# Decayed keys by transposes of scaled keys, the low-rank path's splits moved back, and the inverse's diagonal copies spread out

## The chip, the cores and the metric

The kernel runs on one core of one Trainium2 chip. A core has engines that run side by side, each through its own queue in program order: TensorE (PE in the profile, with its weight loads as PEld), VectorE (DVE), ScalarE (ACT), GpSimd (POOL) and SyncE (SP), which here only issues transfers. TensorE writes into eight banks of accumulators (PSUM), from where VectorE or ScalarE reads the results. The metric is the device time of one execution in microseconds (us), median over runs; lower is better.

## The reference, cut to what matters

The model is a trunk of two layers on 512 positions of 1024 channels: a spatial-gating mixer, a gated feed-forward part with a short convolution, an RWKV-7 mixer, and a second feed-forward part. The change lies in the RWKV-7 mixer:

```python
r = xr @ w_r;  k = xk @ w_k;  v = xv @ w_v
w = -jax.nn.softplus(-(w0 + jnp.tanh(xw @ w1) @ w2)) - 0.5
a = jax.nn.sigmoid(a0 + (xa @ a1) @ a2)
...
decay = jnp.exp(-jnp.exp(heads(w)))
y = wkv7_scan(r_h, decay, k_h, v_h, -kk, kk * a_h)
# step of the scan, per head, state of 64 x 64:
sa = jnp.einsum('bhvk,bhk->bhv', state, a_t)
state = state * w_t[:, :, None, :] + sa[..., None] * b_t[:, :, None, :] + v_t[..., None] * k_t[:, :, None, :]
y_t = jnp.einsum('bhvk,bhk->bhv', state, r_t)
```

There are 16 heads of 64 channels. All is float32 in and out.

## The kernel before, in words

**Arithmetic.** Activations lie with channels on the 128 partitions and the 512 positions along the free axis, so 1024 channels are eight tiles. A large product is split in a high and a low float32r part on each side and done as three matmuls (`mm3`, L311 to L317); `split` (L224 to L239) makes the two parts: ScalarE casts the high one (L234), VectorE subtracts for the low one (L235). Small products are plain float32 matmuls.

**The start of the mixer** is `rwkv_first` (L660 to L723). It computes the low-rank factor of the decay and of `a` for all positions into two accumulators `lw`, then runs four loops `kk` over two input tiles each (L696 to L706), with the receptance weights of the first four output tiles. For each input tile `k` it stores the residual to DRAM (L700), normalizes in place (L701), mixes with the shifted input (`mix`, L647 to L653) and splits the result into `xs[k]`. After the second loop the function `lowrank` (L680 to L691) scales the two accumulators (L683, L684), adds them (L685), takes a tanh of the upper half (L686) and splits both halves into `r.lr` (L690, L691). Then come the other four output tiles in two loops `m` (L711 to L723). `r.lr` is first read in `decay` of the first pair (L853, L855).

**The pairs.** Two heads make one tile of 128 channels, a pair; there are eight (`pairs`, L949 to L974). Time is cut into eight chunks of 64 positions. For each pair `decay` works out the cumulated decay of each chunk (`gt`, its inverse `ei`, and the decay over a whole chunk `gc`), `operands` (L889 to L912) forms `ar`, the decayed queries of both kinds, and `bk`, the two kinds of keys divided by the decay (columns 0 to 63 and 64 to 127 of each chunk; on the lower 64 partitions the first kind is copied behind the second, L912, so that the two heads can have the kinds in opposite order). `products` (L914 to L947) then makes, for two halves of four chunks each, the products of `bk` with `ar` (L928), masks them (L932), copies one quarter into `ti` for the inverse (L933) and stores the rest. At the end it needs the keys times the decay to the chunk's end, with positions and channels exchanged, one per chunk and head. It gets them as a matmul of `bk` with a diagonal matrix `dg` of `gc` (L921, L942), copies them to `bt` (L945) and stores them. Accumulators for `products` come by the names `aux` and `us`, two buffers each, taken in turn; the first of the two heads' results goes to one, the second to the other.

**The inverse.** `invert(g)` (L976 to L1037) inverts, for the four pairs of a half `g`, the unit triangular 64 x 64 matrices of all chunks. It solves the 32 x 32 diagonal blocks on VectorE by 31 steps (L1004, L1005), transposes the blocks (L1010, L1011), copies the inverted diagonal blocks back to `ti` on ScalarE (L1015, four copies), and makes the block off the diagonal by two rounds of 32 x 32 matmuls (L1025 with copies L1035, then L1028 with copies L1037), each in two halves of two portions.

**The scan** (L1160 to L1222) runs over the chunks with `bt`, `ti` and the stored tiles.

**What sets the order.** These parts are Python generators; a `yield` ends a portion. `weave` (L328 to L351) runs the main generator (pairs, later the scan), after each portion as many portions of a side generator (the inverse) and of `fill` as a rate gives. `fill` are the dense projections of keys, values, gates and output, a portion being two input tiles of three matmuls. `issue_after` holds a portion's instructions behind a given instruction on its engine. A scheduler then places the instructions of each engine by order of emission and by its own estimate of when operands and buffers are there, so that an engine's order can differ from the order of the text. On the chip each engine follows that order strictly, and waits where an operand is late.

Of the kernel before, what the change touches and what calls it, by code (L numbers as in the profile page):

```python
# [15 lines left out]
ALU = mybir.AluOpType  # L16
# [4 lines left out]
P = 128  # L21
# [4 lines left out]
C = 64  # L26
NCH = T // C
# [117 lines left out]
class Emit:  # L145
# [514 lines left out]
    def rwkv_first(self, r, ep):  # L660
# [19 lines left out]
        def lowrank():  # L680
            t, u = tmp("lt", 1), tmp("lu", 1, T + 1)
            G.memset(u[:, 0:1], 0.0)
            V.tensor_tensor(t, lw[0], rb, ALU.mult)  # L683
            V.tensor_tensor(u[:, 1:], lw[1], rb, ALU.mult)  # L684
            V.tensor_tensor(t, t, u[:, 0:T], ALU.add)  # L685
            S.activation(t[0:64], t[0:64], AF.Tanh)  # L686

            for j, x in enumerate(r.lr):
                hi, lo = slice(64 * j, 64 * j + 64), slice(64 - 64 * j, 128 - 64 * j)
                S.copy(x[hi], t[hi])  # L690
                V.tensor_tensor(x[lo], t[hi], x[hi].bitcast(F32), ALU.subtract)  # L691


        xs = []
        accs = [self.acc() for _ in range(4)]
        for kk in range(4):  # L696
# [8 lines left out]
            if kk == 1:  # L705
                lowrank()  # L706
        for m in range(4):
# [3 lines left out]
        for m in (0, 2):  # L711
            ws = [self.weights(A["wrb"][m + j]) for j in range(2)]
            if m == 2:
                self.load_l2(0)
            accs = [self.acc() for _ in range(2)]
            for k in range(KT):
                for j in range(2):
                    self.mm3(accs[j], self.wcols(ws[j], k * P, P), xs[k], k == 0, k == KT - 1)
                if m == 2:
                    while len(r.xk) < min(k + 3, KT):  # L720
                        r.xk.append(r.mix(2, len(r.xk)))
            for j in range(2):
                S.copy(r.rt[1][:, m + j, :], accs[j])  # L723

    def rwkv_main(self, r, ctx, gain):
# [3 lines left out]
        H = (h0, h1)  # L729
# [184 lines left out]
        def products(p, u):  # L914


            g, i = divmod(p, 4)
            ar, bk = u.ar, u.bk

            dg = tile_([P, NCH, C], "dg", 1)  # L920
            V.tensor_tensor(dg, self.c("id2", C).unsqueeze(1).to_broadcast([P, NCH, C]), bc(gc[:, p], C), ALU.mult)  # L921
            masks = self.c("masks", P)

            for ch in (slice(0, U), slice(U, NCH)):
# [10 lines left out]
                for hd, o, n, q in ((0, P, P, 0), (0, 2 * P, C, P + C), (1, 0, P + C, C)):  # L935
                    nc.sync.dma_start(std[g][ch, H[hd], i, o:o + n].rearrange("c p t -> p c t"), f[H[hd], :, q:q + n])
                yield
            bt = tile_([P, NCH, 2, C], "bt", BT)
            qs = [self.acc(tag).rearrange("p (c t) -> p c t", t=C) for tag in ("aux", "us")]
            for c in range(NCH):  # L940
                for hd in range(2):
                    nc.tensor.matmul(qs[hd][:, c, :], bk[H[hd], c, C * hd:C * hd + P], dg[H[hd], c, :],  # L942
                                     start=True, stop=True)
            for hd in range(2):
                S.copy(bt[:, :, hd, :], qs[hd])  # L945
            nc.sync.dma_start(btd[:, :, p].rearrange("c p a t -> p c (a t)"), bt.rearrange("p c a t -> p c (a t)"))
# [29 lines left out]
        def invert(g):  # L976
# [35 lines left out]
            yield  # L1012
            off = blocks("tt")
            for rows, cols in Q:
                S.copy(tg[rows, :, cols], y[rows])  # L1015
            for i in range(2):
                for hf in range(2):
                    ps = self.acc("aux").rearrange("p (u t) -> p u t", t=32)
                    us = slice(16 * hf, 16 * hf + 16)
                    for u in range(16):  # L1020
                        for hd in range(2):
# [5 lines left out]
                            else:  # L1027
                                nc.tensor.matmul(ps[b0, u, :], off[b1, n, :], y[b1, n, :], start=True, stop=True,  # L1028
                                                 tile_position=(b1.start, b0.start))
                        if u % 8 == 7:  # L1030
                            yield
                    for hd in range(2):
# [353 lines left out]
```

## Time and profile before

| | |
|---|---|
| median of three runs | 1292.31 us (1291.89 to 1294.6) |
| profiled execution, its own time | 1294.26 us |
| its span, first to last instruction | 1292.4 us |
| mean granted TensorE clock | 0.988 |
| TensorE busy | 98% |
| VectorE busy | 66% |
| ScalarE busy | 49% |

A row of a view by line has the line of the kernel, engine, operation, the tile written, an arrow, the tiles read, how many, then the shortest, median and longest duration in ns, the first and last start in us, and shapes. TensorE rows show weights rows*columns and then the streamed operand. A row of the timeline begins with start and duration in us; in square brackets at its end stands how long the engine had been idle before it, and which instruction ended that. Durations of matmuls contain their latency, so that the time that one costs is read from the distance between two starts. Lines are those of the kernel before.

### The profile page before, as it was taken

What the parts mean: (1) busy time and instruction counts of PE and PEld (TensorE: products, weight loads), DVE (VectorE), ACT (ScalarE), POOL (GpSimd) and SP (SyncE); (2) the same over time, 40 slices, a digit from 0 to 9 for tenths busy, and PEclk for the clock granted to TensorE, in tenths of its full rate; (3) what the DMA queues carried; (4) which work ended last, traced back from release to release, by engine and by line L of the source; (5) the groups of instructions that cost most, each with busy time, mean ns of one, the idle gap of its engine ahead of it and who ended that gap; (6) DMA issues with size and microseconds to landing.
All of it is one profiled execution on the core that took longest, in us unless ns stands there. A gap on an engine that the chain in (4) does not pass through costs nothing.

```text
span 1292.4 us, 19533 instructions
## 1 busy us (share of the span) xinstructions
PE 1269.4 (98%) x7591; PEld 1018.9 (79%) x7591; DVE 852.8 (66%) x1401; ACT 631.3 (49%) x1084; POOL 97.7 (8%) x119
## 2 busy tenths in 40 slices
PE   9999999999999999999999998999999999999997
PEld 6878888888888888787777776677888888888886
DVE  6465468888886444765889587765677777763233
ACT  5534456555554333565785645532544444442222
POOL 4100100000000000000000022231100000000001
PEclk9999999999999999999999998999999999999998
DMA  7332457777557764236878699764233333333332
GB/s 252 102 98 83 129 172 256 245 245 242 175 171 220 217 206 151 90 106 185 224 199 239 171 215 227 193 168 144 78 104 98 98 97 96 93 93 98 90 90 78
DMA packets 115452, 201.65 MB, mean 156 GB/s; under 512 B 21600, under 2 KB 53600, under 8 KB 115360
## 3 DMA queue, kind: packets, MB, share of 16 engines
q10 hardware_dynamic: 39104, 112.87, 29.0%
q1 hardware_dynamic: 76256, 87.54, 23.4%
q8 instruction: 59, 0.97, 0.3%
q14 instruction: 33, 0.27, 0.1%
HBM read 152.93 MB, written 47.45 MB: 155 GB/s over the span
## 4 chain that ended last, share of the span: by engine, by line
PE 88%; DVE 5%; ACT 1%; POOL 0%; issue 0%; DMA 0%; DVEq 0%; ACTq 0%; POOLq 0%
PE mm L315 10%; PE mm L316 9%; PE mm L317 9%; PE aux L315 6%; PE aux L317 6%; PE aux L316 6%; PE e L316 6%; PE e L315 6%; PE e L317 5%; PE us L317 5%; PE us L315 5%; PE us L316 5%; PE aux L928 1%; PE aux L942 1%; PE us L1186 1%; PE us L1199 1%
## 5 line engine op out<-in xcount | busy, mean ns | idle before, releaser
L234 ACT CAST w<-w 128x512 fp32r<-128x512 f32 x340 | 206.3, 610 | 374.3 <-PE aux L317 94.8
L235 DVE TENSOR_TENSOR w<-w,w 128x512 fp32r<-128x512 f32 x340 | 233.3, 688 | 196.7 <-ACT w L234 196.2
L315 PE MATMUL mm<-mxh,w 128*128 128x512 f32 (+1 forms) x416 | 171.7, 414 | 1.6 <-ACT mxh L234 1.6
L316 PE MATMUL mm<-mxl,w 128*128 128x512 f32 (+1 forms) x416 | 166.7, 401 | 0.2 <-DVE mxl L235 0.2
L317 PE MATMUL mm<-mxh,w 128*128 128x512 f32 (+1 forms) x416 | 166.3, 400 | 0.0
L342 POOL TENSOR_TENSOR ss<-ss,sq 128x512 f32<-128x512 f32 x30 | 41.0, 1368 | 777.6 <-issue 595.1
L315 PEld LDWEIGHTS mm<-mxh,w 128*128 128x128 f32 (+1 forms) x416 | 78.2, 189 | 22.0 <-issue 3.3
L317 PEld LDWEIGHTS mm<-mxh,w 128*128 128x128 f32 (+1 forms) x416 | 78.7, 189 | 18.1 <-issue 1.2
L316 PEld LDWEIGHTS mm<-mxl,w 128*128 128x128 f32 (+1 forms) x416 | 78.9, 190 | 16.3 <-issue 1.1
L539 ACT ACTIVATE cv<-z,par 128x512 f32<-128x512 f32 x88 | 71.7, 817 | 28.8 <-DVE z L537 23.8
L315 PE MATMUL us<-mxh,w 128*128 128x512 f32 x216 | 84.6, 392 | 0.0
L315 PE MATMUL aux<-mxh,w 128*128 128x512 f32 x216 | 84.5, 391 | 0.0
L317 PE MATMUL aux<-mxh,w 128*128 128x512 f32 x216 | 84.2, 390 | 0.3 <-DVE w L235 0.3
L316 PE MATMUL aux<-mxl,w 128*128 128x512 f32 x216 | 84.1, 389 | 0.0
L316 PE MATMUL us<-mxl,w 128*128 128x512 f32 x216 | 84.1, 389 | 0.0
L317 PE MATMUL us<-mxh,w 128*128 128x512 f32 x216 | 84.1, 389 | 0.0
L315 PE MATMUL e<-mxh,w 128*128 128x512 f32 x208 | 81.5, 392 | 2.5 <-ACT mxh L234 2.4
L316 PE MATMUL e<-mxl,w 128*128 128x512 f32 x208 | 81.2, 390 | 0.1
L317 PE MATMUL e<-mxh,w 128*128 128x512 f32 x208 | 81.0, 389 | 0.0
L540 DVE SCALAR_TENSOR_TENSOR cv<-z,par,cv 128x512 f32<-128x512 f32 x88 | 66.1, 752 | 19.9 <-ACT cv L539 19.9
L541 DVE SCALAR_TENSOR_TENSOR cv<-z,par,cv 128x512 f32<-128x512 f32 x88 | 66.0, 752 | 2.9
L315 PEld LDWEIGHTS e<-mxh,w 128*128 128x128 f32 x208 | 39.1, 188 | 11.3 <-ACT mxh L234 3.3
(1088 smaller groups left out, 2605.1 us busy)
## 6 DMA issues: line engine op xcount, KB each, us to landing
w<-in_wup ACTq DMA_DIRECT2D x88, 512.0 KB, 3.7
w<-in_wdn ACTq DMA_DIRECT2D x32, 512.0 KB, 3.6
st<-std SPq DMA_DIRECT2D x30, 320.0 KB, 6.9
w<-wkd ACTq DMA_DIRECT2D x16, 512.0 KB, 5.0
w<-wvd ACTq DMA_DIRECT2D x16, 512.0 KB, 5.7
w<-wod ACTq DMA_DIRECT2D x16, 512.0 KB, 4.3
w<-in_wdn ACTq DMA_DIRECT2D x16, 384.0 KB, 3.4
w<-in_wsu ACTq DMA_DIRECT2D x8, 512.0 KB, 3.7
```

The source lines that it names most:

```text
L234: nc.scalar.copy(hi[r, :n], src)
L235: (lo_eng or nc.vector).tensor_tensor(lo[r, :n], src, hi[r, :n].bitcast(F32), ALU.subtract)
L315: mm(acc, wh, xh, start=first, stop=False)
L316: mm(acc, wh, xl, start=False, stop=False)
L317: mm(acc, wl, xh, start=False, stop=last)
L342: nc.gpsimd.tensor_tensor(self.ss, self.ss, self.sq, ALU.add)
L539: nc.scalar.activation(c, z[:, 2:], AF.Identity, scale=cw(2, i), bias=self.p("conv_b", l * 44 + i))
L540: nc.vector.scalar_tensor_tensor(c, z[:, 1:T + 1], cw(1, i), c, ALU.mult, ALU.add)
L541: nc.vector.scalar_tensor_tensor(c, z[:, 0:T], cw(0, i), c, ALU.mult, ALU.add)
L928: nc.tensor.matmul(qs[hd][:, c - ch.start, :], bk[H[hd], c, C * hd:C * hd + P], ar[H[hd], c, :], start=True, stop=True)
L942: nc.tensor.matmul(qs[hd][:, c, :], bk[H[hd], c, C * hd:C * hd + P], dg[H[hd], c, :], start=True, stop=True)
L1186: nc.tensor.matmul(us[H[hd], 0, i, :], ar(i, hd, 0), vu[:, hd, i, :], start=True, stop=True)
```

## The change

There are three edits.

1. `lowrank` becomes a generator. Its first portion (L682 to L684) stays after the second loop `kk`. The sum, tanh and the first split follow after input tile 2 of the next stage's first loop (`m == 0`), the second split after tile 4.
2. In `products` the diagonal `dg` and its 16 matmuls go. Instead VectorE scales `bk` by `gc` into a tile `be`, for four chunks at a time, ScalarE copies one kind of key behind the other on the lower partitions, as for `bk`, and TensorE transposes `be`, chunk by chunk and head by head, against the identity. The scaling of the first half stands at the start of `products`; its transposes and the scaling of the second half stand at the end of the first half; the transposes of the second half stand after the loop. The accumulators of the transposes are taken after the first half.
3. In `invert` the four copies L1015 no longer stand together ahead of the matmuls; one follows each of the four portions of the first round.

```diff
+            yield
             V.tensor_tensor(t, t, u[:, 0:T], ALU.add)
             S.activation(t[0:64], t[0:64], AF.Tanh)
...
                 S.copy(x[hi], t[hi])
                 V.tensor_tensor(x[lo], t[hi], x[hi].bitcast(F32), ALU.subtract)
+                yield
...
-        xs = []
+        xs, low = [], lowrank()
...
             if kk == 1:
-                lowrank()
+                next(low)
...
+                if m == 0 and k in (2, 4):
+                    next(low)
...
-            dg = tile_([P, NCH, C], "dg", 1)
-            V.tensor_tensor(dg, self.c("id2", C).unsqueeze(1).to_broadcast([P, NCH, C]), bc(gc[:, p], C), ALU.mult)
+            id2, qb = self.c("id2", C), []
+
+            def decayed(ch):
+
+                be = tile_([P, U, 3 * C], "be", 1)
+                V.tensor_tensor(be[:, :, 0:P], bk[:, ch, 0:P], bc(gc[:, p, ch], P), ALU.mult)
+                S.copy(be[h1, :, P:], be[h1, :, 0:C])
+                return be
+
+            def turned(ch, be):
+                for c in range(U):
+                    for hd in range(2):
+                        nc.tensor.transpose(qb[hd][:, ch.start + c, :], be[H[hd], c, C * hd:C * hd + P], id2[H[hd]])
+
+            be = decayed(slice(0, U))
...
-                yield
+                if not qb:
+                    qb[:] = [self.acc(tag).rearrange("p (c t) -> p c t", t=C) for tag in ("aux", "us")]
+                    turned(ch, be)
+                    be = decayed(slice(U, NCH))
+                yield
+            turned(slice(U, NCH), be)
             bt = tile_([P, NCH, 2, C], "bt", BT)
-            qs = [self.acc(tag).rearrange("p (c t) -> p c t", t=C) for tag in ("aux", "us")]
-            for c in range(NCH):
-                for hd in range(2):
-                    nc.tensor.matmul(qs[hd][:, c, :], bk[H[hd], c, C * hd:C * hd + P], dg[H[hd], c, :],
-                                     start=True, stop=True)
             for hd in range(2):
-                S.copy(bt[:, :, hd, :], qs[hd])
+                S.copy(bt[:, :, hd, :], qb[hd])
...
-            off = blocks("tt")
-            for rows, cols in Q:
-                S.copy(tg[rows, :, cols], y[rows])
+            off, own = blocks("tt"), iter(Q)
...
                         if u % 8 == 7:
+                            if i == 0:
+                                rows, cols = next(own)
+                                S.copy(tg[rows, :, cols], y[rows])
                             yield
```

## The prediction

> **What bounds the kernel now.** First the page: its header, the busy times and the chain of waits.
>
> ```profile
> span 1292.4 us, 19533 instructions
> PE 1269.4 (98%) x7591; PEld 1018.9 (79%) x7591; DVE 852.8 (66%) x1401; ACT 631.3 (49%) x1084; POOL 97.7 (8%) x119
> PE 88%; DVE 5%; ACT 1%; POOL 0%; issue 0%; DMA 0%; DVEq 0%; ACTq 0%; POOLq 0%
> ```
>
> TensorE is occupied for 98% of the span and carries 88% of the chain, so what is taken off TensorE comes off the end, unless another engine is late at that place. The whole-span shares hide that, so the second view is the table of stretches (duration, then PE, PEld, DVE, ACT, POOL busy with instruction counts, the granted TensorE clock, DMA share, GB/s).
>
> ```profile
> 600.00:680.00 80.00, 80.00 (x636) 61.82 (x635) 65.94 (x115) 58.64 (x110) 0.56 (x5) 1.00 0.78 216
> 680.00:700.00 20.00, 19.86 (x152) 15.49 (x151) 18.16 (x46) 12.10 (x27) 0.11 (x1) 0.91 0.76 216
> 700.00:723.00 23.00, 22.54 (x150) 16.99 (x146) 21.77 (x51) 10.77 (x24) 0.61 (x2) 1.00 0.97 272
> 600.00:723.00 123.00, 122.39 (x933) 94.30 (x931) 105.86 (x211) 81.51 (x159) 1.28 (x8) 0.99 0.81 227
> 723.00:740.00 17.00, 16.94 (x303) 14.30 (x303) 6.44 (x9) 11.51 (x18) 0.00 (x0) 0.94 0.47 122
> ```
>
> The eight pairs run from 600 to 740. TensorE is full throughout, but VectorE is at 65.94 of 80 up to 680 (14.1 us free), 18.16 of 20 after it, and 21.77 of 23 in 700 to 723 (1.2 us free), where it also runs the first inverse's substitution. There VectorE sets the pace as much as TensorE.
>
> **The decayed keys: TensorE's part.** The change removes 16 products of keys with a diagonal per pair (L942) and adds 16 transposes. By line, all over the span, with the nearest transposes the kernel has (L1239: 32 of them, so one record each, where the 128 products of L942 make 256 records, two each):
>
> ```profile
> L942 PE MATMUL aux<-dg,bk x128: 218/272/320, 615.9 to 736.6; 64*128 64x64 f32 x128
> L942 PE MATMUL us<-dg,bk x128: 218/272/320, 615.9 to 736.4; 64*128 64x64 f32 x128
> L1239 PE MATMUL aux<-cst,y x32: 271/273/328, 773.4 to 887.2; 128*128 128x128 f32 x32
> 615.88 0.32 PE L942 MATMUL aux<-dg,bk 64*128 64x64 f32 x1
> 617.81 0.51 PE L315 MATMUL mm<-mxh,w 128*128 128x512 f32 x1
> 773.43 0.60 PE L1239 MATMUL aux<-cst,y 128*128 128x128 f32 x4
> ```
>
> One pair's 32 records hold TensorE from 615.88 to 617.81: 1.93 us, 0.060 a record, since the two heads' records run side by side; eight pairs make 15.4. The new 128 transposes have the same weights' shape (64 rows, 128 columns) and the same two heads. At one record each and the same 0.060 they take 7.7, so 7.7 is saved. The trace shows no transpose on half the rows: if two heads' transposes do not run side by side, each costs what an L1239 one does, (0.60 - 0.27)/3 = 0.11 us, 128 of them 14.1, and only 1.3 is saved. The value 0.060 is taken, because the shape is that of L942 and only the identity differs.
>
> A group of 64-row instructions also pays at its edges:
>
> ```profile
> 621.44 0.39 PE L316 MATMUL mm<-mxl,w 128*128 128x512 f32 x1
> 621.67 0.39 PE L317 MATMUL mm<-mxh,w 128*128 128x512 f32 x1
> 621.99 0.37 PE L928 MATMUL aux<-ar,bk 64*128 64x128 f32 x1
> 622.20 0.27 PE L928 MATMUL aux<-ar,bk 64*128 64x128 f32 x1
> 622.31 0.27 PE L928 MATMUL aux<-ar,bk 64*128 64x128 f32 x1
> ```
>
> The last dense product before it takes 0.32 to the next start and not 0.23, the first pair of records 0.21 and not 0.11; with as much at the end (I assume symmetry) it is some 0.38 a group. The single group becomes two half groups, each following a group of L928 in program order. Both standing alone cost 8 x 0.38 = 3.0 more, both joined to L928 give 3.0 back; I take nothing. TensorE saves 7.7, bounds 1.3 - 3.0 = -1.7 (a loss) and 10.7.
>
> The trace agrees on the records with the Trainium skill, "TensorE: Matmul & The Clock Gate", section Terms: it gives the chip's transpose mode as four times faster for FP32. By that 15.4 would fall to an estimated 3.9 and 11.6 be saved; the spacing of 0.11 at L1239 does not show so much, so I stay with the half.
>
> **Its cost on VectorE and ScalarE.**
>
> ```profile
> L921 DVE TENSOR_TENSOR dg<-cst,gc x8: 684/685/693, 601.3 to 716.1; 128x512 f32<-128x512 f32 x8
> L933 ACT COPY ti<-lq x32: 392/404/408, 607.5 to 734.1; 64x256 f32<-64x256 f32 x32
> L932 DVE TENSOR_TENSOR lq<-us,cst x16: 646/681/692, 607.4 to 729.9; 128x512 f32<-128x512 f32 x16
> L945 ACT COPY bt<-aux x8: 562/586/587, 617.9 to 736.9; 128x512 f32<-128x512 f32 x8
> ```
>
> The diagonal (0.685) goes; two scalings of 4 chunks x 128 columns, again 128x512, come: 8 x 0.685 = 5.5 us more on VectorE. Two copies of 64x256 a pair come on ScalarE: 16 x 0.404 = 6.5. ScalarE has 41 us free in 600 to 723 and hides them. VectorE has 123 - 105.9 = 17.1 free, 14.1 of it before 680; five pairs' 3.4 us are hidden there by TensorE's dense products. After 680 they are not: of the two pairs around 690 to 716 TensorE's saving (2 x 0.96 = 1.9) is lost, because VectorE has next to nothing free there, and 2 x 0.685 = 1.4 is added. The DMA share of 0.97 there speaks the same way: the weights could hardly come sooner. Net of the transposes: 7.7 - 1.9 - 1.4 = 4.4 us gained; if the cover also fails before 680, 3.4 less and the rest of the saving with it.
>
> The accumulators are held longer: the transposes' two stay from the first half of a pair to its end, so the second half's products wait for the masks on the first half (L932, two of 0.68), and the next pair's first products for the copies out (L945, two of 0.59). With one buffer for the scaled keys, VectorE's second scaling waits for the first transposes, and the next operand work queues behind it. Dense products between these places cover them, as the second pair shows, whose second half starts after the masks on the first have ended:
>
> ```profile
> 623.38 0.68 DVE L932 TENSOR_TENSOR lq<-aux,cst 128x512 f32<-128x512 f32 x1
> 623.98 0.68 DVE L932 TENSOR_TENSOR lq<-us,cst 128x512 f32<-128x512 f32 x1
> 625.75 0.37 PE L928 MATMUL aux<-ar,bk 64*128 64x128 f32 x1
> ```
>
> So they are costed at nothing; uncovered they are 1.4 + 1.2 = 2.6 us a pair.
>
> **The low-rank path.** TensorE's one long wait before the pairs, with VectorE's row of work in front of it:
>
> ```profile
> 545.02 0.39 PE L317 MATMUL aux<-mxh,w 128*128 128x512 f32 x1
> 547.81 0.50 PE L315 MATMUL e<-mxh,w 128*128 128x512 f32 x1 [2.40 <-ACT mxh L234]
> 540.02 0.68 DVE L685 TENSOR_TENSOR lt<-lt,lu 128x512 f32<-128x512 f32 x1
> 541.83 0.68 DVE L235 TENSOR_TENSOR w<-w,w 128x512 fp32r<-128x512 f32 x1
> 543.00 1.39 DVE L691 TENSOR_TENSOR lr<-lt,lr 64x512 fp32r<-64x512 f32 x2 [0.50 <-ACT lr L690]
> 544.42 1.42 DVE L701 SCALAR_TENSOR_TENSOR h<-h,par,rb 128x512 f32<-128x512 f32 x2
> 541.71 1.26 ACT L690 CAST lr<-lt 64x512 fp32r<-64x512 f32 x2
> ```
>
> From 545.02 to 547.81 is 2.79 us where 0.23 is normal: 2.56 lost. TensorE waits for xs[4], whose first step is L701 at 544.42, queued behind L691, which waited for ScalarE's L690. The change takes L685, the tanh and L690/L691 away from there. VectorE's last work then ends at 541.83 + 0.68 = 542.51 and L701 starts 1.9 us earlier, 2.56 if the split moves up by L685's 0.68 as well. I take 2.2. The two pieces (L685, then L691 in two parts: 2.07 us of VectorE, and tanh and L690, 1.9 of ScalarE) go between dense products of the next loop, which cover them; their reader is the first pair's decay, after two loops of dense products. Bounds: 0, if they stall the next splits as they stall these, and 2.56. No DMA is among them.
>
> **The inverse's copies.** In the second inverse ScalarE has L1015 in front of the operand that TensorE waits for:
>
> ```profile
> 796.73 0.69 DVE L1047 SCALAR_TENSOR_TENSOR sq<-h,omu,sq 128x512 f32<-128x512 f32 x1
> 796.87 1.04 ACT L1015 COPY ti<-li 32x1024 f32<-32x1024 f32 x1 [1.51 <-DVE li L1011]
> 797.82 0.61 ACT L234 CAST mxh<-sq 128x512 fp32r<-128x512 f32 x1
> 798.48 0.72 PE L315 MATMUL mm<-mxh,w 128*128 128x512 f32 x2 [1.56 <-ACT mxh L234]
> ```
>
> Its input is ready at 797.42, the cast starts at 797.82. Later copies free 0.4; one copy's 1.04 either way bounds it, as a copy may now stand in front of another reader.
>
> **The sum.** 2.2 + 4.4 + 0.4 = 7.0 us. The profiled execution took 1294.26 us (1.9 around its span of 1292.4), which gives 1287.3. It was 1.95 slower than the median of the runs, 1292.31, which the new median will be compared with: 1285.3, forecast 1285.5.
>
> **The rivals.**
>
> *VectorE is the bound in all pairs.* For: 14.1 us free before 680 are spread over waits that TensorE's order makes. Against: 3.4 needed. Then transposes bring nothing and 2.6 remains: 1289.7, up to 1291 with the 1.4.
>
> *The transposes are not cheaper* (no side by side, edges paid): -1.7 and -1.4, against 2.6: 1292.8.
>
> *A slow spell of the clock goes.* With small instructions packed, the clock was halved for what followed:
>
> ```profile
> 734.57:737.99 3.42, 3.42 (x76) 3.18 (x68) 0.66 (x1) 1.08 (x3) 0.00 (x0) 1.00 0.37 90
> 737.99:748.23 10.24, 10.24 (x86) 8.08 (x86) 2.14 (x1) 6.13 (x11) 2.36 (x4) 0.50 0.65 156
> ```
>
> In 737.99 to 748.23 it is 0.50, which costs 5.1 us. Before it lie small products, the last pair's L942 among them; with half as many records dense work moves in. Then 1280.2. Against: the inverse's 32-row products stay.
>
> *Slower by the accumulators:* the waits of 2.6 us a pair stand on TensorE because its order puts the second half right behind the first. It decides from 0.9 us a pair on, which eats the 7.0; in full 8 x 2.6 = 20.8 - 7.0: slower by 13.8, at half by 3.4, 1296. Against: in the second pair 1.09 us lie between the masks' end at 624.66 and the second half.
>
> *Slower by the clock:* transposes count little as work, and a spell of 3.41 us at 0.50 follows in each pair, 1.7 us: from four pairs on nothing is gained; eight make 13.6 - 7.0 = 6.6, 1299. The rows above bear it out as far as full occupation (3.42 of 3.42) did not keep the clock. The Trainium skill, "TensorE: Matmul & The Clock Gate", Part 4, says just this of transposes: they do not count as busy as other products do. Against: in a pair dense products surround them, and L942's group left the clock at 1.00 up to 680.
>
> **How the numbers follow.** Forecast 0.52 (1282 to 1289.5), spell gone 0.17, VectorE 0.10, transposes dear 0.05 with 0.05 for mixtures that end near 1291, accumulators 0.06, clock 0.05. The runs tell no change from one of 0.2%, 2.6 us: faster is below 1289.7, slower above 1294.9. Faster: 0.52 + 0.17 + half of VectorE's = 0.74; same 0.15; slower 0.11. The range 1278.5 to 1292 leaves out the last two, part of the dear transposes and little below.
>
> **What would show it.** One record per transpose, and pairs of them 0.11 to 0.12 apart; the wait at 547.81 gone or under 0.7; the first pairs closer together by some 0.7 us each, the last two not; no wait of TensorE's products for L932 or L945 over 0.5. Two records per transpose, or the clock at 0.50 inside the pairs, would make the prediction wrong.

## The result

The changed kernel takes 1299.68 us (median of 11 runs, 1296.19 to 1306.66). The kernel before, run beside it, takes 1292.31 us (median of 11, 1291.23 to 1296.61). The ratio is 1.0052, with a 95% interval of 1.004 to 1.0064: the change made the kernel slower by half a per cent, where 1285.5 us and faster had been forecast, and 1299.68 lies above the range's end of 1292.

The profiled execution after took 1300.81 us, 6.55 more than the one before (1294.26). Of the changed kernel's page, the header, the busy times and the chain by engine:

```profile
span 1299.0 us, 19310 instructions
PE 1273.2 (98%) x7463; PEld 1017.7 (78%) x7463; DVE 857.4 (66%) x1409; ACT 638.2 (49%) x1100; POOL 98.7 (8%) x119
PE 86%; DVE 5%; ACT 2%; DMA 1%; issue 1%; POOL 0%; DVEq 0%; ACTq 0%; POOLq 0%
```

TensorE has 128 records fewer (7463 for 7591), as 256 became 128, yet it is occupied for 3.8 us longer, and its share of the chain fell from 88% to 86%. So TensorE's work did not shrink, and some waits are new. Where they are, the table of stretches of the changed kernel says (duration; PE, PEld, DVE, ACT, POOL busy with counts; granted clock; DMA share; GB/s):

```profile
540.00:548.00 8.00, 7.98 (x35) 6.07 (x34) 8.00 (x14) 5.14 (x10) 0.00 (x0) 1.00 0.28 74
600.00:680.00 80.00, 78.88 (x525) 57.60 (x523) 63.16 (x110) 57.82 (x110) 0.56 (x5) 0.96 0.73 199
680.00:700.00 20.00, 18.06 (x128) 13.17 (x127) 16.46 (x38) 12.99 (x27) 0.11 (x1) 0.98 0.65 181
700.00:723.00 23.00, 23.00 (x124) 17.55 (x124) 18.65 (x42) 12.98 (x30) 0.61 (x2) 0.87 0.77 217
600.00:723.00 123.00, 119.94 (x774) 88.33 (x772) 98.27 (x189) 83.79 (x165) 1.29 (x8) 0.94 0.73 200
```

In the low-rank path's stretch, 540 to 548, TensorE is now full: the stall there is gone. In the pairs it is the other way. In the same 123 us TensorE gets through 774 records instead of 933, 159 fewer where the change itself takes at most 128 away, and VectorE has become *less* busy, 98.3 instead of 105.9: by its share it is not the bound. TensorE is at 18.06 of 20 in 680 to 700, and the weights' transfers fell back with it (200 GB/s instead of 227).

The landmarks place the loss. The first copy of the receptance's first loop, right behind the low-rank path, starts at 554.4 and not 557.4; here are these rows by line, first of the kernel before, then of the changed one (shortest, median, longest in ns, then first and last start):

```profile
L708 ACT COPY rt<-e x1: 587/587/587, 557.4 to 557.4; 128x512 f32<-128x512 f32 x1
```

```profile
L710 ACT COPY rt<-e x1: 589/589/589, 554.4 to 554.4; 128x512 f32<-128x512 f32 x1
L902 DVE TENSOR_TENSOR ar<-kn,gt x8: 651/685/693, 590.7 to 702.4; 128x512 f32<-128x512 f32 x8
L961 ACT COPY bt<-aux x8: 562/576/593, 615.6 to 744.1; 128x512 f32<-128x512 f32 x8
```

L902 opens the operands of each pair, L961 closes the pairs. Before, the first pair's operands began at 593.8, the last one's at 696.7, and the last `bt` copy started at 736.9. So the change was 3.0 us ahead at the first pair, 5.7 us behind at the last one, and 7.2 behind at the end of the pairs.

To see what that time consists of, I kept a ledger for the stretch from the first pair's operands to the scan's first copy of V. From the time that passes, three things are taken: the loss by halved clock (half the length of each spell at a granted clock of 0.50), the time that TensorE idled, and 0.2275 us for each of the 290 dense products in it, which is the distance between the starts of two dense products in a row. The rest is what the *small* products cost TensorE: their own time, the edges of their groups, and the gaps that the profile doesn't count as idle.

| us | passes | halved clock | TensorE idle | 290 dense products | small products |
|---|---|---|---|---|---|
| before | 156.56 | 6.83 | 0.67 | 65.98 | 83.1 |
| after | 162.81 | 6.83 | 5.02 | 65.98 | 85.0 |

The loss in this stretch, 6.25 us, is 4.35 of new idle time and 1.9 of small products, which were to become 7.7 cheaper. Halved clock takes the same 6.83 us in both. The largest waits in the 5.02 us of idle time are 1.7 for a scaling (L928) and 1.6 for a copy on ScalarE that belongs to another part of the mixer (L839). The sum over the whole span closes: -3.04 up to the first pair, +6.25 here, +3.38 in the scan, where 6.8 us more at half the clock (13.65 against 6.83) cost 3.4, and -0.04 behind it make 6.55.

### Why the transposes are not cheap

By line, the changed kernel's transposes (two rows, one for each head's accumulator), the scaling that feeds them and its copy:

```profile
L935 PE MATMUL aux<-cst,be x64: 216/223/273, 604.6 to 739.3; 64*128 64x64 f32 x64
L935 PE MATMUL us<-cst,be x64: 215/223/273, 609.4 to 740.3; 64*128 64x64 f32 x64
L928 DVE TENSOR_TENSOR be<-bk,gc x16: 662/690/694, 598.3 to 738.1; 128x512 f32<-128x512 f32 x16
```

One record per transpose and 0.69 us for a scaling are as forecast. But the first head's transposes begin at 604.6 and the second head's at 609.4. TensorE's timeline of the changed kernel, at one pair's half and around the place of its longest wait:

```profile
612.61 0.39 PE L317 MATMUL mm<-mxh,w 128*128 128x512 f32 x1
612.92 0.46 PE L935 MATMUL aux<-cst,be 64*128 64x64 f32 x4
613.32 0.50 PE L315 MATMUL mm<-mxh,w 128*128 128x512 f32 x1
613.65 0.40 PE L316 MATMUL mm<-mxl,w 128*128 128x512 f32 x1
...
614.22 0.46 PE L935 MATMUL us<-cst,be 64*128 64x64 f32 x4
...
691.37 1.16 PE L944 MATMUL aux<-ar,bk 64*128 64x128 f32 x8
692.46 1.13 PE L841 MATMUL mm<-rt,wb 128*128 128x512 f32 x2
693.52 0.46 PE L935 MATMUL us<-cst,be 64*128 64x64 f32 x4
693.82 1.11 PE L944 MATMUL us<-ar,bk 64*128 64x128 f32 x8
696.63 0.46 PE L935 MATMUL aux<-cst,be 64*128 64x64 f32 x4 [1.71 <-DVE be L928]
```

A row with x4 is four records in a row with nothing of the other head between them. The two heads no longer stand side by side: the first head's four transposes at 612.92 are followed by dense work, the second head's four come at 614.22. Such a group of four costs TensorE 0.58 us over the dense products around it (612.61 to 613.65 is 1.04 for two dense products' 0.46). A pair has four such groups, 2.3 us, where the old single group of 32 records had 1.93, or 2.1 when its edges are counted in the same way (in the pair at 659.18, 2.59 with two dense products). So nothing is saved. The products of keys and queries came apart in the same way: eight records of one head at 691.37 take 1.09 us to the next start, as long as sixteen with the heads side by side (610.26 to 611.36 in the same trace).

I counted in the traces, as lone, each record beside which none of the other head starts within 25 ns. Before, 40 of 256 product records and 34 of 256 records of L942 were lone; after, 128 of 256 and 112 of the 128 transposes (14 of the 16 half groups; in the other two the heads do stand side by side).

### The profile page after: what moved, and what is told of

Its sections match the earlier page's. It is cut to its first block, busy times and chain, and to the rows that moved or that the text cites. A ratio compares the mean times of both kernels' runs of the same rounds, so it can differ in the third digit from the quotient of the medians.

```text
span 1299.0 us, 19310 instructions
## 1 busy us (share of the span) xinstructions
PE 1273.2 (98%) x7463; PEld 1017.7 (78%) x7463; DVE 857.4 (66%) x1409; ACT 638.2 (49%) x1100; POOL 98.7 (8%) x119
## 4 chain that ended last, share of the span: by engine, by line
PE 86%; DVE 5%; ACT 2%; DMA 1%; issue 1%; POOL 0%; DVEq 0%; ACTq 0%; POOLq 0%
PE mm L315 9%; PE mm L316 9%; PE mm L317 9%; PE aux L315 6%; PE aux L317 6%; PE aux L316 6%; PE e L316 6%; PE e L315 6%; PE e L317 6%; PE us L316 5%; PE us L315 5%; PE us L317 5%; PE aux L944 1%; PE e L889 1%; PE us L1216 1%; PE us L1203 1%
## 5 line engine op out<-in xcount | busy, mean ns | idle before, releaser
L317 PEld LDWEIGHTS aux<-mxh,w 128*128 128x128 f32 x216 | 40.6, 188 | 9.3 <-DVE w L235 0.8
```

The lines of the kernel that those rows point to most:

```text
L317: mm(acc, wl, xh, start=False, stop=last)
```

## The experiments

Each run's time was also freed of the clock: less (1 - mean granted clock) times its span, the median of this over the runs. It supposes that the span follows the clock, and with a clock given to 0.001 one run is good to about 0.65 us. What the clock costs is, below, the median less this figure. "Before" was run beside each set and came to 1292.31, 1293.83 (beside e1, e2, e4 and e5), 1293.18 (e3, e6, e7) and 1292.77 us (e8, e9, e10). Without the clock's loss the last three are 1278.0, 1278.7 and 1278.55, so that the clock costs the kernel before 14.2 to 15.8 us.

| kernel | median us | ratio to before (95%) | without clock loss | lone products, of 256 | lone transposes, of 128 (diagonal products, of 256) |
|---|---|---|---|---|---|
| before | 1292.31 | 1 | 1278.0 to 1278.7 | 40 | (34) |
| after | 1299.68 | 1.0052 (1.004 to 1.0064) | 1282.3 | 128 | 112 |
| e1_lowrank | 1290.55 | 0.9979 (0.9967 to 0.9991) | 1275.7 | 40 | (34) |
| e2_turn | 1305.64 | 1.0101 (1.0087 to 1.0116) | 1284.5 | 128 | 112 |
| e3_inverse | 1291.07 | 0.9984 (0.9974 to 0.9994) | 1279.0 | 36 | (34) |
| e4_heads | 1298.78 | 1.0047 (1.0035 to 1.0059) | 1277.6 | 78 | 8 |
| e5_end | 1290.41 | 0.9988 (0.9968 to 1.0007) | 1274.8 | 36 | 16 |
| e6_placed | 1294.74 | 1.0016 (0.9994 to 1.0038) | 1279.2 | 46 | (54) |
| e7_pool | 1302.93 | 1.0066 (1.0048 to 1.0085) | 1278.3 | 38 | 20 |
| e8_unscaled | 1290.11 | 0.9975 (0.9966 to 0.9984) | 1272.8 | 78 | 16 |
| e9_aside | 1298.23 | 1.0039 (1.0026 to 1.0052) | 1277.0 | 72 | 22 |
| e10_both | 1287.27 | 0.9952 (0.9939 to 0.9965) | 1275.7 | 36 | (34) |

The ledger of the pairs, as above, of the profiled executions that are spoken of below (290 dense products, 65.98 us, in each but e6 and e9, which have 291 and 294):

| us | passes | halved clock | TensorE idle | small products |
|---|---|---|---|---|
| before | 156.56 | 6.83 | 0.67 | 83.1 |
| after | 162.81 | 6.83 | 5.02 | 85.0 |
| e4_heads | 159.15 | 8.53 | 7.01 | 77.6 |
| e5_end | 151.38 | 3.41 | 10.40 | 71.6 |
| e6_placed | 152.85 | 0 | 2.38 | 84.3 |
| e7_pool | 159.64 | 10.24 | 11.34 | 72.1 |
| e8_unscaled | 154.27 | 8.53 | 4.72 | 75.0 |
| e9_aside | 158.75 | 10.24 | 7.76 | 73.9 |
| e10_both | 151.06 | 0 | 1.30 | 83.8 |

### One edit at a time: e1_lowrank, e2_turn, e3_inverse

Each is the kernel before with one of the three edits, exactly as the change has it.

```diff
# e1_lowrank: the three hunks of lowrank and rwkv_first alone
+            yield
             V.tensor_tensor(t, t, u[:, 0:T], ALU.add)
...
+                if m == 0 and k in (2, 4):
+                    next(low)
# e2_turn: the hunks of products alone
-            dg = tile_([P, NCH, C], "dg", 1)
...
+            be = decayed(slice(0, U))
...
+            turned(slice(U, NCH), be)
# e3_inverse: the hunks of invert alone
+                            if i == 0:
+                                rows, cols = next(own)
+                                S.copy(tg[rows, :, cols], y[rows])
```

> The kernel before with the first edit alone (low-rank path in three portions). Both theories: the wait of 2.4 us at the start of the mixer goes, as it does in the trace after; 1289.3 against 1292.3 before. If what the later stages lose comes from the shift in time of everything behind (other phase of the clock's halving) and not from the transposes, this kernel loses it too and stands at 1295 or more.

> The kernel before with the second edit alone (transposes of scaled keys). If the transposes carry the whole loss, 1299.7 + 3.0 = 1302 to 1303, and about 112 of 128 transpose records and about 128 of 256 product records run without the other head's record beside them, as in the trace after (before: 34 and 40 of 256). If the loss came with the other two edits: 1292 or less.

> The kernel before with the third edit alone (the inverse's diagonal copies between the portions). All theories: within 0.2% of before, 1291 to 1296; the first edit gave 0.21% and the second cost 1.01%, the change as a whole cost 0.52%, so if the edits simply add, this one would have to give 0.28%, 1290.

Each is taken against the kernel before beside it. The low-rank edit brings 0.2% (2.3 us without the clock's loss), the inverse's copies 0.2% in the runs, but nothing once the clock is taken out (+0.3). The transposes cost 1.0%, 12 us, 6.5 of it at full clock. The three differences at full clock add up to +4.5 (-2.3 + 6.5 + 0.3), and the changed kernel's own is +3.6 to +4.3 (1282.3 against 1278.0 to 1278.7). So, as far as the rounding tells, the edits don't hinder each other, and the whole loss comes with the transposes.

### The two heads held together: e4_heads

The changed kernel, with the transposes of a half held behind the first one of the second head (its operand comes last), so that the heads alternate. No other line changes.

```diff
             def turned(ch, be):
+                with ExitStack() as behind:
                 for c in range(U):
-                    for hd in range(2):
+                    for hd in (1, 0):
                         nc.tensor.transpose(qb[hd][:, ch.start + c, :], be[H[hd], c, C * hd:C * hd + P], id2[H[hd]])
+                        if c == 0 and hd == 1:
+                            behind.enter_context(tc.issue_after(self.last(mybir.EngineType.PE)))
```

> The changed kernel, with each half's eight transposes held behind the first one of the second head, so that the two heads' transposes go side by side. Theory 'heads apart': some 112 lone records at 0.10 become pairs, and 36 groups become about 16 at 0.38 a group: 5 us or more back, 1294 to 1295. Theory 'accumulators held': the products of keys and queries stay as split as they are (128 lone records), 1298 to 1300. Theory 'VectorE': no change, 1299.7.

TensorE's timeline of this kernel, where a half's transposes begin:

```profile
609.06 0.39 PE L317 MATMUL mm<-mxh,w 128*128 128x512 f32 x1
609.38 0.27 PE L936 MATMUL us<-cst,be 64*128 64x64 f32 x1
609.38 0.27 PE L936 MATMUL aux<-cst,be 64*128 64x64 f32 x1
609.49 0.22 PE L936 MATMUL us<-cst,be 64*128 64x64 f32 x1
609.49 0.22 PE L936 MATMUL aux<-cst,be 64*128 64x64 f32 x1
...
609.68 0.33 PE L947 MATMUL us<-ar,bk 64*128 64x128 f32 x1
609.68 0.33 PE L947 MATMUL aux<-ar,bk 64*128 64x128 f32 x1
```

Now eight transposes take 609.38 to 609.68, 0.30 us, and the products right behind them run in pairs too. With dense products on both sides eight take 0.40 us (613.48 to 613.88), the same as four of one head alone took. Lone transposes fell from 112 to 8, lone products from 128 to 78. Without the clock's loss the kernel is 4.6 us faster than the changed one, and in the ledger the small products went from 85.0 to 77.6. So it is shown that the heads' coming apart costs about this much. The measured median is another matter: 1298.78 is only 0.9 below the changed kernel, with overlapping intervals and short of the 1294 to 1295 expected, since this version loses 21 us to the clock where the changed one loses 17.4. In the profiled executions, of the 7.4 us gained on small products 2.0 go to more idle time of TensorE (7.0 us in the stretch), 1.7 to more halved clock in the stretch and 3.4 to more halved clock in the scan.

### All transposes at the end, accumulators taken only there: e5_end

The keys are scaled in place behind each half's products, and all 16 transposes of a pair stand in one group behind both halves, as the old products with the diagonal did; the accumulators are taken there. As in e4 the group is held behind the second head's first transpose, and here the chunks are taken from the last to the first. So this run changes the place, the tile and the order together.

```diff
-                be = tile_([P, U, 3 * C], "be", 1)
-                V.tensor_tensor(be[:, :, 0:P], bk[:, ch, 0:P], bc(gc[:, p, ch], P), ALU.mult)
-                S.copy(be[h1, :, P:], be[h1, :, 0:C])
+                V.tensor_tensor(bk[:, ch, 0:P], bk[:, ch, 0:P], bc(gc[:, p, ch], P), ALU.mult)
+                S.copy(bk[h1, ch, P:], bk[h1, ch, 0:C])
...
-            def turned(ch, be):
...
+            def turned():
+                with ExitStack() as behind:
+                    for c in reversed(range(NCH)):
+                        for hd in (1, 0):
+                            nc.tensor.transpose(qb[hd][:, c, :], bk[H[hd], c, C * hd:C * hd + P], id2[H[hd]])
+                            if c == NCH - 1 and hd == 1:
+                                behind.enter_context(tc.issue_after(self.last(mybir.EngineType.PE)))
...
-            be = decayed(slice(0, U))
...
-                if not qb:
-                    qb[:] = [self.acc(tag).rearrange("p (c t) -> p c t", t=C) for tag in ("aux", "us")]
-                    turned(ch, be)
-                    be = decayed(slice(U, NCH))
+                decayed(ch)
                 yield
-            turned(slice(U, NCH), be)
+            qb[:] = [self.acc(tag).rearrange("p (c t) -> p c t", t=C) for tag in ("aux", "us")]
+            turned()
```

> The changed kernel, with the keys scaled in place after their half's products, and all 16 transposes of a pair in one group at the end, where alone their accumulators are taken. VectorE and ScalarE do the same work as in the changed kernel. Theories 'heads apart' and 'accumulators held': both the lone transposes and the lone products go back to the number before (34 to 40), and the saving shows: one group of 8 pairs of records, 0.9 + 0.38 against 2.2 us a pair, 7 us, with the 3.0 of the low-rank path: 1283 to 1287. Theory 'VectorE' (5.5 us more work where it is the bound): 1297 to 1300. Theory 'clock' (transposes do not count as work): the clock is halved inside the pairs still.

TensorE's timeline of this kernel, from a group's first to its last records and the product behind it:

```profile
613.92 0.27 PE L934 MATMUL us<-cst,bk 64*128 64x64 f32 x1
613.93 0.27 PE L934 MATMUL aux<-cst,bk 64*128 64x64 f32 x1
614.03 0.22 PE L934 MATMUL us<-cst,bk 64*128 64x64 f32 x1
...
614.42 0.22 PE L934 MATMUL us<-cst,bk 64*128 64x64 f32 x1
614.57 0.88 PE L889 MATMUL e<-cst,n 128*64 128x128 f32 x12
```

Sixteen transposes take 0.65 us, pairs of them 0.063 apart: where the heads do stand side by side, a transpose costs 0.03 to 0.04, where the prediction took 0.060, and a pair's 16 a third of the 1.93 us before. In the ledger the small products fall by 11.5 us (83.1 to 71.6), more than the 7.7 forecast: the transposes are cheaper than priced, and the products of keys and queries have kept their partners (36 lone). But the stretch passes only 5.2 us sooner, and 3.4 of that is the clock's: TensorE idles 10.4 us instead of 0.67. Its stretches show where:

```profile
600.00:723.00 123.00, 112.60 (x869) 85.24 (x869) 110.14 (x215) 85.90 (x170) 1.29 (x8) 0.97 0.78 220
640.00:665.00 25.00, 19.98 (x147) 15.38 (x145) 22.01 (x37) 20.03 (x38) 0.11 (x1) 0.86 0.55 142
```

TensorE is busy 19.98 of 25 us in 640 to 665, with VectorE at 22.01. The longest single wait there, in the waits of TensorE from 580 to 750 (what waited, for what, total us, times, longest), is for a step of `decay`, which prepares a later pair:

```profile
PE e L881 <- ACT sq L871: 5.3, 2, 5.0
```

So with the transposes cheap, TensorE runs ahead and meets the other engines' pace; over all, e5 ties with the kernel before (0.9988, interval 0.9968 to 1.0007) although it has the low-rank gain in it, and misses the 1283 to 1287 expected.

### The accumulators alone: e6_placed

The kernel before, with its old products with the diagonal, but in two halves at the change's places, and so with the accumulators held from the first half on. No edit of the other two.

```diff
+            def turned(ch):
+                for c in range(ch.start, ch.stop):
+                    for hd in range(2):
+                        nc.tensor.matmul(qb[hd][:, c, :], bk[H[hd], c, C * hd:C * hd + P], dg[H[hd], c, :],
+                                         start=True, stop=True)
...
+                if not qb:
+                    qb[:] = [self.acc(tag).rearrange("p (c t) -> p c t", t=C) for tag in ("aux", "us")]
+                    turned(ch)
                 yield
+            turned(slice(U, NCH))
```

> The kernel before, its products with the diagonal kept, but taken in two halves at the places where the changed kernel has its transposes, into accumulators held from the end of the first half. No scaled keys, no more VectorE or ScalarE work. Theory 'accumulators held': half of the records lose their partner here too (100 or more lone product records of 256, before 40) and the time is 1298 to 1303. Theory 'heads apart through the copy of one head's keys': both heads' operands are ready together, so pairs stay pairs and only the one more group a pair is paid, 3 us: 1295 to 1297. Theory 'VectorE': as before, 1292 to 1294.

The runs are 0.16% slower, an interval that holds 1, and 0.5 to 1.2 us slower at full clock, which the clock's rounding can make. Lone records hardly rise (46 and 54). So neither the halves nor the held accumulators part the heads. What remains is readiness: the operands of the two heads come ready one after the other, since ScalarE's copy (L929) stands before the second head's, and the diagonal products needed only `bk` and `dg`, which are ready long before. That last step is argued, and the changed kernel's trace bears it out only in part. Of its 14 half groups that came apart, five have the first head's transposes start before the copy for the second head had ended. In the other nine the copy too had ended before either head's transposes began, as for the group at 612.92, whose copy ended at 611.14:

```profile
610.74 0.40 ACT L929 COPY be<-be 64x256 f32<-64x256 f32 x1 [0.93 <-DVE be L928]
```

There nothing forced the heads apart at run time on this account: the order of the instructions was already so. Why the scheduler placed them so, by its own estimate of when operands are there or for another reason, no run shows. Shown are that holding for the later head joins the heads, and that accumulators don't part them.

### What TensorE meets once the transposes are cheap: e7_pool, e8_unscaled, e9_aside

All three are e5_end with one thing changed: the scaling given to GpSimd; the scaling and its copy left out, so that undecayed keys are transposed; the scaling and copy done, but into a tile that nobody reads, the undecayed keys being transposed.

```diff
# e7_pool
-                V.tensor_tensor(bk[:, ch, 0:P], bk[:, ch, 0:P], bc(gc[:, p, ch], P), ALU.mult)
+                G.tensor_tensor(bk[:, ch, 0:P], bk[:, ch, 0:P], bc(gc[:, p, ch], P), ALU.mult)
# e8_unscaled
-                decayed(ch)
# e9_aside
-                V.tensor_tensor(bk[:, ch, 0:P], bk[:, ch, 0:P], bc(gc[:, p, ch], P), ALU.mult)
-                S.copy(bk[h1, ch, P:], bk[h1, ch, 0:C])
+                be = tile_([P, U, P], "be", 1)
+                V.tensor_tensor(be, bk[:, ch, 0:P], bc(gc[:, p, ch], P), ALU.mult)
+                S.copy(be[h1, :, 0:C], be[h1, :, C:P])
```

> The changed kernel with the transposes of a pair in one group at the end, as in the run with 1290.4, and the scaling of the keys on GpSimd in place of VectorE (11 us less on VectorE than there, 5.5 less than before the change). Theory 'VectorE is the bound once the heads are together': of the 10.4 us that TensorE idled in the pairs there 7 or more go, 1281 to 1285. Rival 'readiness': GpSimd takes twice as long for a scaling (1.37 us for a 128x512 sum), the transposes wait for it, and the time is 1289 to 1295.

> As the run with all 16 transposes of a pair in one group at the end (1290.4), but the keys are not scaled: the scaling and the copy behind it are left out, and the transposes take the undecayed keys. Leaves 11 us of VectorE's and 6.5 us of ScalarE's work out. Theory 'VectorE or the wait for the scaled keys is next': of the 10.4 us that TensorE idled there in the pairs most goes, 1281 to 1284. Theory 'order': the idle time comes from the place of the pairs' other work, and stays, 1288 to 1292.

> As the run without scaling, but the scaling and its copy are done into a tile that nobody reads, so that VectorE and ScalarE work as much as in the run with 1290.4, and no transpose waits for them. Theory 'VectorE is the bound once the heads are together': TensorE idles 8 us or more in the pairs, 1289 to 1292. Rival 'readiness': it idles little, as without scaling, 1281 to 1285.

The scaling on GpSimd, by line, and the longest of TensorE's waits in 580 to 760, both of e7_pool:

```profile
L927 POOL TENSOR_TENSOR bk<-bk,gc x16: 1040/1042/1752, 604.2 to 738.0; 128x512 f32<-128x512 f32 x16
```

```profile
PE us L934 <- ACT bk L928: 5.3, 3, 4.1
PE mm L315 <- DVE rt L843: 4.1, 2, 3.1
```

Taking 16 scalings off VectorE did not help: TensorE idles 11.3 us in the stretch, 5.3 of it for the copy behind the scaling and 4.1 for a step on VectorE (L843). At 1302.93 us the kernel is slower than both ranges expected. GpSimd takes longer for a scaling, so this is no clean test of VectorE's load; it shows that a scaling that is late for its group is enough to make TensorE idle. Without any scaling (e8) 4.7 us of idle remain, with the scaling done aside (e9) 7.8, at 1298.23 us, again above both ranges expected. Read as steps, of e5's 10.4 us some 4.7 come from the order alone, 3.0 from VectorE's and ScalarE's work, and 2.6 from the transposes' waiting for it. But the order of e8 and of e9 has fallen apart again (78 and 72 lone products, where e5 has 36), so these shares are not settled and stay open. Even with no scaling at all, e8 takes 1290.11 us, more than e10_both below, which keeps the diagonal. At full clock it is the other way: e8 is 2.9 us below e10, but it leaves the scaling out. e5 is 3.2 below the kernel before beside it, where e1, beside the same one, is 2.3 and e10, beside its own, 2.9 below. So the transposes' net gain at full clock is 0.9 us at most, hardly clear of the rounding, and the clock took it back.

### The two good edits alone: e10_both

The kernel before with the low-rank edit and the inverse's copies; the products with the diagonal stay. Its diff is that of e1_lowrank and of e3_inverse together.

> The kernel before with the first and the third edit, and its products with the diagonal. If the edits add and the transposes carry the whole loss: 0.21% and 0.16% less than before, 1288 to 1289, faster than both kernels.

Its page's header and busy times, and its stretch of the pairs:

```profile
span 1282.7 us, 19533 instructions
PE 1262.7 (98%) x7591; PEld 1013.8 (79%) x7591; DVE 851.5 (66%) x1401; ACT 631.2 (49%) x1084; POOL 98.3 (8%) x119
```

```profile
600.00:723.00 123.00, 122.34 (x1028) 94.28 (x1029) 106.60 (x209) 82.93 (x161) 1.29 (x8) 1.00 0.79 225
```

1287.27 us, a ratio of 0.9952 (0.9939 to 0.9965): faster than both kernels. TensorE is as full in the pairs as before (122.34 of 123), and the clock stays at 1.00 there. At full clock it gains about what e1 gains (2.9 us against the kernel before beside it, 1278.55); the rest, 2.6 us, is the clock, which cost less in these runs.

## Why the prediction was wrong, point by point

**The low-rank path: right.** 2.2 us were forecast, with 2.56 as the most; the landmark behind it moved by 3.04 and e1 measured 2.3 at full clock. TensorE's 5.60 of 8 in 540 to 548 became 7.98. Up to the first pair TensorE idled 5.8 us before and 2.7 after: 2.40 of this is the one gap that the bound had counted, and 0.54 is a shorter wait at 5.5 us, at the kernel's start, where the edit changes nothing.

```profile
540.00:548.00 8.00, 5.60 (x25) 4.32 (x24) 7.46 (x13) 6.15 (x11) 0.11 (x1) 1.00 0.22 66
```

This row is the kernel before's: 2.40 us of idle time in 8 us, of which 0.02 are left. The two pieces of `lowrank` stalled nothing at their new place.

**The inverse's copies: nothing.** 0.4 was forecast and the sign can't be told at full clock. The 0.2% that its runs show came with a smaller loss by the clock (12.1 us against 14.5 for the kernel before beside it).

**The transposes: the step that failed.** It is "The value 0.060 is taken, because the shape is that of L942 and only the identity differs", together with "I take nothing" for the groups' edges. Both assume that two heads' transposes run side by side in one group. The shape allows that, as e5's 0.063 a pair shows; but it happens only where the two heads' records follow each other in TensorE's order, and that had changed too: 112 of 128 ran alone. The likely reason, argued and not shown, is that the diagonal products read `bk`, complete long before, and the transposes read `be`, whose second head waits for one more copy on ScalarE. The lower bound, -1.7, did count lone transposes and paid edges, but only for one thing: it left out that the *products* of keys and queries beside them lose their partners with them (40 lone to 128), and that TensorE's order, once torn, waits (0.67 us idle to 5.02). The edit cost 6.5 us at full clock (e2) where between a gain of 10.7 and a loss of 1.7 had been allowed on TensorE and a net gain of 4.4 was taken. Holding the heads together brings 4.6 of them back (e4). The forecast's sign was lost in this term.

On the transposes' records themselves the trace agrees with the Trainium skill, "TensorE: Matmul & The Clock Gate", Part 3, which has matmuls on different row groups run concurrently, with starts about 4 ns apart. In e4 and e5 the two heads' records start 0.00 to 0.01 us apart, as finely as these rows tell. Lone, a transpose showed 0.10 us (four in 0.40). Side by side a pair took 0.063, where two products of L942 took two pairs of records 0.11 apart, 0.22; with the groups' edges, 16 took 0.65 where the old ones took 1.93. That is between a quarter and a third of the old price, and only when side by side. The Trainium skill, "TensorE: Matmul & The Clock Gate", section Terms, calls the transpose mode four times faster for FP32, and the estimate by that rule, which I set aside in the prediction, was nearer to the records side by side than my half.

**VectorE's part: wrong in its place.** VectorE was to lose 1.9 + 1.4 us for TensorE after 680. In the changed kernel VectorE has more free time there than before (16.46 of 20, 18.65 of 23). What it does show is a single wait of 1.71 us for a scaling (696.63). The bound that I looked for appears only when the transposes are really cheap, in e5, and before 680.

**The rivals.** *Transposes not cheaper* (chance 0.05, 1292.8) named the right cause, "no side by side, edges paid", and missed the size, by leaving the products and the idle time out. *Accumulators held* (0.06) falls, though its sign shows once: in the changed kernel TensorE's matmuls wait for the masks (L948) in two places, 0.6 and 0.2 us, the first just above the 0.5 named as a sign, and its weight loads 2.7 us in all, 0.8 at most. For the copies out a weight load waits 0.4 once. That is little of the 5.02 us of idle time, and e6 shows no cost beyond the measurement.

```profile
PEld aux L935 <- DVE be L928: 1.9, 1, 1.9
PEld aux L935 <- DVE lq L948: 1.3, 4, 0.4
PEld us L944 <- DVE lq L948: 0.8, 1, 0.8
```

These are the longest of the waits for the scalings and the masks among TensorE's weight loads in 600 to 760 of the changed kernel. *Slower by the clock* (0.05, 1299) gave the right number by luck, for a reason that the runs don't bear out: transposes as such need not cost clock. e5 has all 128 of them and loses 15.6 us to the clock, the kernel before beside it 15.8, and e6, without any, 15.5. The Trainium skill's sentence that they do not count as busy in the same way ("TensorE: Matmul & The Clock Gate", Part 4) is thus not seen to matter here. In the changed kernel the spells at half the clock come behind stretches in which TensorE idles:

```profile
657.00:665.00 8.00, 7.01 (x46) 5.17 (x44) 7.97 (x16) 5.36 (x12) 0.00 (x0) 1.00 0.62 180
665.00:671.80 6.80, 6.67 (x27) 4.84 (x27) 5.95 (x11) 5.18 (x11) 0.11 (x1) 0.50 0.71 150
692.00:699.10 7.10, 5.16 (x41) 3.82 (x40) 6.61 (x15) 5.14 (x11) 0.00 (x0) 1.00 0.46 118
699.10:705.90 6.80, 6.80 (x22) 5.69 (x22) 6.13 (x15) 2.93 (x7) 0.00 (x0) 0.50 0.69 195
```

Idle times of 1.0 of 8 and 1.9 of 7.1 us stand ahead of the two spells. So the loss by the clock, 17.4 us against 14.2 to 15.8, comes on top of the waits, and may be their result; that is argued from these rows, not shown by a run that takes away the waits alone. Against it, the kernel before has two spells among its pairs as well, one of them behind a stretch without any idle time (734.57 to 737.99, in the prediction). *The spell goes* and *VectorE bounds all pairs*: neither happened.

**What would have shown it.** The list of signs was good for the records and the low-rank wait, and it had the right one for this failure, the distance between pairs. It asked for pairs 0.11 to 0.12 apart; of 64 pairs the trace has 8, in two half groups, and the rest are lone records. The sign against the prediction, the clock at 0.50 inside the pairs, is there too (665.0 and 699.1), but the kernel before shows it as well.

## What to carry to other kernels

When small matmuls on half the rows are priced by a group in which two heads run side by side, the price holds only if the new records of both heads still follow each other in the engine's order. Look for that order in the trace, ask which engine's step stands before each head's operand, and hold the earlier head for the later one if needed. Price also the neighbours that are torn apart with them, and the queue that then has to feed an engine that runs ahead: here the 16 transposes could be had for 0.65 us instead of 1.93, and the kernel as a whole still got no faster than with the old products. And a part that brings 0.2% should be tried alone: the two small edits without the large one are the fastest kernel of this study, though only the low-rank one shows a gain at full clock.

## What the hardware showed that I had not expected

Transposes of 64 rows side by side cost 0.063 us a pair, where the records they replace cost 0.11 a pair and came twice as often. Between dense products, eight lone product records of one head take 1.09 us, as long as eight of each head side by side; four lone transposes take 0.40, as long as four of each head side by side. GpSimd takes 1.04 us for the 128x512 scaling, VectorE 0.69. And the run-to-run spread of one kernel goes with its clock: one run of e5_end took 1286.06 us at a mean granted clock of 0.992, another 1302.07 at 0.977; 0.015 of the span would be 19.5 us, more than the 16.0 between them.
